# Where the sums of the sevenfold chunks are made: a hybrid decoder layer on one core

## The chip, the core and the metric

The kernel runs on one core of one Trainium2 chip. The time is the device time of one execution in microseconds (us), and the figure compared is the median of several runs. TensorE is written PE (its weight loads PEld), VectorE DVE, ScalarE ACT, GpSimd POOL, SyncE SP. Everything is computed in float32. A DMA that SP or ACT issues is on that engine's queue; the transfers of all queues run on the same 16 DMA engines of the core.

## The reference

One decoder layer for 256 tokens and a model width of 2048. Cut to what matters:

```python
def reference(x, ...):
    h = rmsnorm(x, norm_mix_pre)
    proj = h @ w_in                        # 2048 -> xr, yr, q, k, v, two gates
    y_rnn = rg_lru(conv(xr)) * gelu(yr)
    y_att = sliding_window_sink_attention(rope(q), rope(k), v, sinks)   # 32 heads of 64, 4 kv heads
    mix = sigmoid(g_rnn) * (y_rnn @ w_rnn_proj) + sigmoid(g_attn) * (y_att @ w_attn_proj)
    x = x + rmsnorm(mix @ w_out, norm_mix_post)
    h = rmsnorm(x, norm_mlp_pre)
    u = square(relu(h @ w_mlp_up))         # 2048 -> 8192
    return x + rmsnorm(u @ w_mlp_down, norm_mlp_post)   # 8192 -> 2048
```

## The kernel before, in words

**Weights as a stream.** Every weight matrix is cut into chunks of 128 partitions x 2048 floats (1 MB). `Stream` (from line 52) brings the chunks one after another, in halves of 1024 columns: `load_to` issues a half's DMA on SP's queue (L73) into a buffer `wraw` (four of them, 512 KB each), and `split_to` makes two parts of it, a high part `whi` (ACT, L91) and the low rest `wlo` (DVE, L92), since PE multiplies in three products of two-part numbers: high x high, high x low, low x high. Six halves of parts exist at a time. A `wraw` buffer is free for the next load when its `wlo` is made.

**Stages.** Three input projections with attention and the recurrence between them (to about 735 us), the projection `w_out` with the norms behind it (to about 850 us), then twice (f = 0, 1): up projection, 16 pairs of chunks (`a_pair`, L234 and L237), and down projection in two passes of 1024 output columns (`down`, `n` = 0, 1; matmuls at L908). The last pass ends with the norm and the output.

**Sevenfold chunks.** A chunk of the down projection multiplies a 256 x 256 block of `u` (2 x 2 tiles of 128 x 128) with a 256 x 1024 block of weights (2 x 2 tiles of 128 x 512). The plain way has 8 tile products, 24 matmuls of 512 columns. For the chunks in `SEVEN` (0, 2, 4, 6, 8, 10, 12 of 16 in each of the four passes, 28 in all) a scheme with 7 products of sums of tiles is used, 21 matmuls. The sums of `u`'s tiles are made once by `evacuate` (L888 to L903). The sums of the weights' tiles are made by DVE when the chunk's turn comes (`split_sums`): three additions (L104, L106, L107) make four sums, one of them in place; then come the splits of the chunk's two halves (L91, L92) and of the 1536 columns beside them (ACT L110, DVE L111).

**Attention.** For each of 4 groups of heads and each of two blocks of tokens, the scores `sc` are matmuls over 64 rows: the even heads lie in partitions 0 to 63, the odd ones in 64 to 127. All matmuls of one half (`par`) come first, then those of the other (L527).

**What sets the order.** A scheduler lays out each engine's instructions by data dependencies and the order in which the code is traced. `tc.issue_after(i)` orders what is traced inside behind instruction `i` if both are on one engine, and adds no wait.

Of the kernel before, what the change touches and what calls it, by code (L numbers as in the profile page):

```python
# [16 lines left out]
F32 = mybir.dt.float32  # L17
# [17 lines left out]
WRAW, WHALF, T2, HELD = 4, 6, 8, 4  # L35

SEVEN = (0, 2, 4, 6, 8, 10, 12)
PAIRS = 16
# [13 lines left out]
class Stream:  # L52
# [3 lines left out]
    def __init__(self, nc, pool, chunks, room, sums):  # L56
        self.nc, self.pool, self.chunks, self.room, self.sums = nc, pool, chunks, room, sums
        self.raw, self.parts = {}, {}
        self.loaded = self.split = 0
        self.pin = lambda i: i  # L60
        self.at = 0

    def load_to(self, n):
        while self.loaded < min(n, 2 * len(self.chunks)):
            j = self.loaded
            c = slice(j % 2 * 1024, j % 2 * 1024 + 1024)
            if j < 2 * EXTRA:
                if j % 2 == 0:
                    self.place = self.room(f"wraw{j}")
                t = self.place[:, c]  # L70
            else:
                t = self.pool.tile([P, 1024], F32, tag="wraw", bufs=WRAW, name=f"wraw{j}")
            self.nc.sync.dma_start(t, self.chunks[j // 2][:, c])  # L73
            self.raw[j] = t
            self.loaded += 1

    def split_to(self, n):
        while self.split < min(n, 2 * len(self.chunks)):
            j = self.split
            if j // 2 in self.sums:  # L80
                self.split_sums(j)
                self.split += 2
                continue
            self.load_to(j + 1)
            self.parts[j] = self.two_parts(self.raw.pop(j), j)
            self.split += 1

    def two_parts(self, src, j):
        hi = self.pool.tile([P, 1024], F32R, tag="whi", bufs=WHALF, name=f"whi{j}")
        lo = self.pool.tile([P, 1024], F32R, tag="wlo", bufs=WHALF, name=f"wlo{j}")  # L90
        self.pin(self.nc.scalar.copy(hi, src))  # L91
        self.pin(self.nc.vector.tensor_tensor(lo, src, hi.bitcast(F32), ALU.subtract))  # L92
        return hi, lo

    def split_sums(self, j):


        self.load_to(j + 2)
        v = self.nc.vector
        a, b = self.raw.pop(j), self.raw.pop(j + 1)  # L100
        t = self.room(f"t{j}")[:, 0:1536]
        hi, lo = [self.room(f"t{part}{j}").bitcast(F32R)[:, 0:1536] for part in ("hi", "lo")]
        one, two, l, r = t[:, 0:1024], t[:, 1024:1536], slice(0, 512), slice(512, 1024)
        v.tensor_tensor(one.rearrange("p (a b) -> p a b", a=2), b[:, l].unsqueeze(1).to_broadcast([P, 2, 512]),  # L104
                        a.rearrange("p (a b) -> p a b", a=2), ALU.add)
        v.tensor_tensor(b[:, l], t[:, l], a[:, r], ALU.add)  # L106
        v.tensor_tensor(two, b[:, l], b[:, r], ALU.add)  # L107
        ahi, alo = self.two_parts(a, j)
        bhi, blo = self.two_parts(b, j + 1)
        self.nc.scalar.copy(hi, t)  # L110
        v.tensor_tensor(lo, t, hi.bitcast(F32), ALU.subtract)  # L111
        parts = {"B11": (ahi[:, l], alo[:, l]), "B22": (ahi[:, r], alo[:, r]), "T2": (bhi[:, l], blo[:, l]),
                 "B21": (bhi[:, r], blo[:, r])}
        for i, name in enumerate(("T1", "T3", "T4")):
            c = slice(i * 512, i * 512 + 512)
            parts[name] = hi[:, c], lo[:, c]
        self.parts[j] = parts

    def ahead(self, j):
        self.split_to(j + AHEAD)  # L120
        self.load_to(max(2 * EXTRA, j + WHALF) + WRAW)

    def half(self, run_ahead=True):
        j = self.at
        self.at += 1
        if run_ahead:
            self.ahead(j)
        else:
            self.split_to(j + 1)
        return self.parts.pop(j)  # L130

    def seven(self):

        j = self.at
        self.at += 2
        self.ahead(j)
        return self.parts.pop(j)
# [4 lines left out]
AHEAD = 6  # L142
HELD_LAST = 5
# [6 lines left out]
def layer(tc, x, pos_t, pos_row, inv_freq, vecs, sinks, gains, w_kv, w_q, w_xy, w_rg, w_g, w_rp, w_ap, w_out,  # L150
# [9 lines left out]
    pairs = [psa, psa]  # L160

# [22 lines left out]
    chunks += [w_out[i] for i in range(16)]  # L184
    sums = set()
    for f in range(2):
        chunks += [w_up[32 * f + i] for i in range(32)]
        for n in range(2):
            sums.update(len(chunks) + i for i in SEVEN)
            chunks += [w_dn[(2 * f + n) * PAIRS + i] for i in range(PAIRS)]  # L190

# [6 lines left out]
    ws = Stream(nc, wpool, chunks, lambda name: flat(unit(name, F32)), sums)  # L198
# [25 lines left out]
    def a_pair(acts, out):  # L224


        ps = pair("ps")
        for f in range(2):
            both = ps[:, f].rearrange("p a b -> p (a b)")
            for half in range(2):  # L230
                hi, lo = ws.half()
                act = [acts[kt // 4][:, kt % 4] for kt in range(half * 8, half * 8 + 8)]
                for k, a in enumerate(act):
                    mm(both, hi[:, k * P : k * P + P], a.rearrange("p a b -> p (a b)"),  # L234
                       start=half == 0 and k == 0, stop=False)
                for k, a in enumerate(act):
                    mm(ps[:, f, 1, :], lo[:, k * P : k * P + P], a[:, 0, :], start=False,  # L237
                       stop=half == 1 and k == 7)
                pump()
        nc.scalar.copy(out, ps[:, :, 1, :])  # L240
        nc.vector.tensor_tensor(out, ps[:, :, 0, :], out, ALU.add)

# [13 lines left out]

    def b_pass512(acts, name):

        banks = [[bank(psb, f"{name}{tb}")] for tb in range(TB)]
        for j in range(8):  # L260
            hi, lo = ws.half()
            for i in range(2):
                c = slice(i * 512, i * 512 + 512)
                b_step(banks, acts, 2 * j + i, hi[:, c], lo[:, c], 2 * j + i == KT - 1)
            if j % 2:
                pump()
        return [b[0] for b in banks]
# [31 lines left out]
    def quarter(q):  # L299
        return slice(q * 512, q * 512 + 512)  # L300

    for q in range(4):
        last = nc.sync.dma_start(x_nat[0][:, quarter(q)], x_v[0][:, quarter(q)])
    with tc.issue_after(last.ins):
        ws.load_to(2)
        for q in range(4):
            last = nc.sync.dma_start(x_nat[1][:, quarter(q)], x_v[1][:, quarter(q)])
    with tc.issue_after(last.ins):
        ws.load_to(2 * EXTRA + WRAW)
# [56 lines left out]
    def kv_step(j, hi, lo, tbs):  # L366
        for i in range(2):
            c = slice(i * 512, i * 512 + 512)
            b_step(kv, hT, 2 * j + i, hi[:, c], lo[:, c], 2 * j + i == KT - 1, tbs)
# [14 lines left out]
    held = [ws.half(False) for j in range(2)]  # L384
# [5 lines left out]
    kv_step(0, *held[0], (0,))  # L390
# [5 lines left out]
    kv_step(1, *held[1], (0,))  # L396
# [8 lines left out]
    kv_step(0, *held[0], (1,))  # L405
# [5 lines left out]
    kv_step(1, *held[1], (1,))  # L411
    for j in range(2, 8):
        if j == 4:
            ws.pin = lambda i: i
        kv_step(j, *ws.half(), (0, 1))
# [80 lines left out]
    def attention(g, banks):  # L496
# [11 lines left out]
        for tb in range(TB):  # L508
# [12 lines left out]
            for par in range(2):  # L521
                r0 = par * HD
                for j in range(4 // per):
                    ps = bank(psm, "sc")
                    for i in range(per):
                        h = j * per + i
                        mm(ps[:, i * w : i * w + w], qT[r0 : r0 + HD, h, tb * P : tb * P + P],  # L527
                           kT[r0 : r0 + HD, g, 0:w], start=True, stop=True)
                    at = par * 4 + j * per
# [24 lines left out]
            for par in range(2):  # L554
                for kb in range(nk):
                    ps = bank(psm, "pt")
                    for h in range(4):
                        s3, at = tiles[par * (4 // per) + h // per]
# [94 lines left out]
    def gates(m):  # L653
        hold = []
        for n in (2 * m, 2 * m + 1):
            hi, lo = ws.half()
# [103 lines left out]
    away = ctx2.enter_context(tc.tile_pool(name="away", bufs=1, space=bass.MemoryType.DRAM))  # L760
# [16 lines left out]
    def b_pass1024(acts, n_kt, name, finish, n_held=HELD):  # L777

        banks = [[bank(psb, f"{name}{tb}{i}") for i in range(2)] for tb in range(TB)]
        for kt in range(n_kt - n_held):  # L780
            hi, lo = ws.half()
            b_step(banks, acts, kt, hi, lo, False)
        held = [(kt,) + ws.half(False) for kt in range(n_kt - n_held, n_kt)]
# [6 lines left out]
        if name == "o1":  # L790
            with tc.issue_after(order[1, AFTER][0]), tc.issue_after(order[1, AFTER][1]):
                ws.ahead(ws.at - 1)
        else:
            ws.ahead(ws.at - 1)
# [92 lines left out]
    def evacuate(p, u, dst):  # L887
# [3 lines left out]
        if p not in SEVEN:  # L891
# [13 lines left out]
    def product(b, a, w, begun, tail=False):  # L905

        for i, (x, y) in enumerate(((0, 0), (0, 1), (1, 0))):
# [3 lines left out]
    LEFT = {"P1": (0, "B11"), "Q3": (6, "B22"), "P2": (2, "B21"), "P6": (5, "T2"), "Q4": (1, "T4"), "Q5": (4, "T1"),  # L911
            "N7": (3, "T3")}
# [3 lines left out]
    def down(f, n, uT, held, order, finish, early):  # L916
# [8 lines left out]
        def step(p, parts, names):  # L925
            for name in names:
                at, n2 = name
                b = PLACE[name]
                for i, (hi, lo) in enumerate(parts):
# [198 lines left out]
```

## Time and profile before

| | |
|---|---|
| Median of 3 runs | 1554.8 us (1554.32 to 1557.64) |
| The profiled execution, its own time | 1553.58 us |
| Its span in the profile | 1551.8 us |
| Mean granted PE clock | 0.993 |
| Instructions | 20974 |
| Time busy: PE, DVE, ACT | 1525.7, 1117.5, 843.9 us |
| Bytes moved by DMA | 296.26 MB, mean 191 GB/s |

The profile is of one execution. Its page gives busy times, DMA queues, the chain of work that ended last and the groups of instructions by line; the trace behind it answers for single stretches (windows: busy time per engine, DMA share and GB/s) and for single instructions (timeline: start, duration, engine, line, shape). Matmul durations overlap, since one starts before the one ahead has drained: what a matmul costs is read from the distance of two starts.

### The profile page before, as it was taken

How to read it: one execution, taken by the hardware profiler on the slowest of the kernel's cores; microseconds unless marked ns; L12 is line 12 of the kernel's file. 1: busy time of each engine (PE TensorE's matmuls, PEld its weight loads, DVE VectorE, ACT ScalarE, POOL GpSimd, SP SyncE). 2: the span in 40 equal slices, each digit the busy share in tenths (PEclk: the TensorE clock that was granted, in tenths of full speed). 3: DMA queues.
4: the chain of work that ended last, by engine and by line, in shares of the span. 5: the costliest groups of instructions: out<-in, count | busy, mean ns of one | idle time of the engine just before them, and what ended most of it. 6: DMA issues, size and time to landing. Idle time of an engine off the chain costs nothing.

```text
span 1551.8 us, 20974 instructions
## 1 busy us (share of the span) xinstructions
PE 1525.7 (98%) x8042; PEld 1295.5 (83%) x8042; DVE 1117.5 (72%) x1364; ACT 843.9 (54%) x1156; POOL 1.7 (0%) x9
## 2 busy tenths in 40 slices
PE   8999999999999999999999999999999999999997
PEld 6887777888888888888787888888888888888885
DVE  6666666866859877555655866688886666788997
ACT  5555545646647766444344655555454555555553
POOL 0000000000000000000000000000000000000000
PEclk9999999999999999999999999999999999999999
DMA  6554354354655465555663855556666655566664
GB/s 246 188 169 148 115 173 147 124 191 149 229 188 177 158 213 198 190 184 190 250 221 98 278 190 189 187 175 213 218 203 218 221 187 189 188 242 232 203 216 138
DMA packets 82902, 296.26 MB, mean 191 GB/s; under 512 B 9585, under 2 KB 9841, under 8 KB 81777
## 3 DMA queue, kind: packets, MB, share of 16 engines
q1 hardware_dynamic: 79344, 285.48, 55.7%
q10 hardware_dynamic: 3458, 9.45, 1.6%
q8 instruction: 63, 1.03, 0.3%
q14 instruction: 37, 0.30, 0.1%
HBM read 288.60 MB, written 6.29 MB: 190 GB/s over the span
## 4 chain that ended last, share of the span: by engine, by line
PE 87%; DVE 5%; ACT 3%; DMA 3%; issue 2%; SPq 0%; DVEq 0%; ACTq 0%
PE ps L234 36%; PE ps L237 18%; PE dQ L908 7%; PE s L908 4%; PE dP L908 3%; DVE wlo L92 2%; PE dCs L908 2%; DMA wraw<-in_w_dn 2%; PE o L251 2%; PE o L255 2%; PE o L253 2%; PE q L251 2%; PE q L253 2%; PE q L255 2%; PE sc L527 1%
## 5 line engine op out<-in xcount | busy, mean ns | idle before, releaser
L92 DVE TENSOR_TENSOR wlo<-wraw,whi 128x1024 fp32r<-128x1024 f32 x528 | 639.8, 1221 | 322.4 <-ACT whi L91 317.0
L91 ACT CAST whi<-wraw 128x1024 fp32r<-128x1024 f32 x528 | 549.0, 1049 | 585.9 <-PE ps L234 271.5
L234 PE MATMUL ps<-hT,whi 128*128 128x512 f32 x1024 | 260.5, 394 | 0.0
L234 PE MATMUL ps<-h2T,whi 128*128 128x512 f32 x1024 | 258.2, 394 | 0.5 <-DVE h2T L280 0.5
L234 PEld LDWEIGHTS ps<-hT,whi 128*128 128x128 f32 x1024 | 183.8, 189 | 36.5 <-issue 3.5
L234 PEld LDWEIGHTS ps<-h2T,whi 128*128 128x128 f32 x1024 | 185.3, 190 | 34.2 <-DVE h2T L280 0.9
L237 PEld LDWEIGHTS ps<-hT,wlo 128*128 128x128 f32 x1024 | 140.1, 190 | 11.7 <-issue 2.0
L237 PEld LDWEIGHTS ps<-h2T,wlo 128*128 128x128 f32 x1024 | 140.0, 191 | 10.1
L237 PE MATMUL ps<-hT,wlo 128*128 128x256 f32 x1024 | 145.3, 283 | 0.0
L237 PE MATMUL ps<-h2T,wlo 128*128 128x256 f32 x1024 | 143.0, 283 | 0.0
L908 PE MATMUL dQ<-whi,uT 128*128 128x512 f32 x288 | 106.5, 389 | 0.0
L234 PE MATMUL ps<-yrnn,whi 128*128 128x512 f32 x256 | 64.4, 393 | 0.7 <-DVE yrnn L700 0.7
L234 PE MATMUL ps<-yatt,whi 128*128 128x512 f32 x256 | 64.1, 392 | 0.0
L908 PEld LDWEIGHTS dQ<-whi,uT 128*128 128x128 f32 x288 | 54.1, 188 | 11.2
L908 PE MATMUL dQ<-wlo,uT 128*128 128x512 f32 x144 | 56.1, 390 | 1.6 <-DVE wlo L92 1.6
L111 DVE TENSOR_TENSOR tlo<-t,thi 128x1536 fp32r<-128x1536 f32 x28 | 49.2, 1757 | 10.1 <-ACT thi L110 10.1
L908 PE MATMUL dP<-whi,uT 128*128 128x512 f32 x144 | 53.8, 389 | 0.0
L908 PE MATMUL dCs<-whi,uT 128*128 128x512 f32 x144 | 53.7, 389 | 0.0
L234 PEld LDWEIGHTS ps<-yrnn,whi 128*128 128x128 f32 x256 | 46.0, 189 | 9.3 <-DVE yrnn L700 1.1
L234 PEld LDWEIGHTS ps<-yatt,whi 128*128 128x128 f32 x256 | 46.0, 189 | 8.2
L251 PE MATMUL q<-whi,hT 128*128 128x512 f32 x128 | 51.1, 399 | 0.0
L253 PE MATMUL q<-wlo,hT 128*128 128x512 f32 x128 | 50.2, 392 | 0.0
(251 smaller groups left out, 2068.6 us busy)
## 6 DMA issues: line engine op xcount, KB each, us to landing
wraw<-in_w_up SPq DMA_DIRECT2D x128, 512.0 KB, 4.6
wraw<-in_w_dn SPq DMA_DIRECT2D x128, 512.0 KB, 4.5
wraw<-in_w_g SPq DMA_DIRECT2D x64, 512.0 KB, 4.4
wraw<-in_w_xy SPq DMA_DIRECT2D x64, 512.0 KB, 3.9
wraw<-in_w_q SPq DMA_DIRECT2D x32, 512.0 KB, 4.3
wraw<-in_w_ap SPq DMA_DIRECT2D x32, 512.0 KB, 3.8
wraw<-in_w_rp SPq DMA_DIRECT2D x32, 512.0 KB, 4.6
wraw<-in_w_out SPq DMA_DIRECT2D x32, 512.0 KB, 4.8
```

Source lines behind the costliest of these rows:

```text
L91: self.pin(self.nc.scalar.copy(hi, src))
L92: self.pin(self.nc.vector.tensor_tensor(lo, src, hi.bitcast(F32), ALU.subtract))
L111: v.tensor_tensor(lo, t, hi.bitcast(F32), ALU.subtract)
L234: mm(both, hi[:, k * P : k * P + P], a.rearrange("p a b -> p (a b)"), start=half == 0 and k == 0, stop=False)
L237: mm(ps[:, f, 1, :], lo[:, k * P : k * P + P], a[:, 0, :], start=False, stop=half == 1 and k == 7)
L251: mm(banks[tb][n], a[:, 0, t], hi[:, n * 512 : n * 512 + 512], start=first, stop=False)
L253: mm(banks[tb][n], a[:, 0, t], lo[:, n * 512 : n * 512 + 512], start=False, stop=False)
L255: mm(banks[tb][n], a[:, 1, t], hi[:, n * 512 : n * 512 + 512], start=False, stop=last)
L527: mm(ps[:, i * w : i * w + w], qT[r0 : r0 + HD, h, tb * P : tb * P + P], kT[r0 : r0 + HD, g, 0:w], start=True, stop=True)
L908: mm(b, a[x], w[y], start=not begun and i == 0, stop=tail and i == 2)
```

## The change

1. **Sums in DRAM.** The seven operands of a sevenfold chunk are now loaded as two pieces: three quarters as they are (1536 columns, from the weights) and four sums (2048 columns) from a DRAM room `sums`. POOL's queue fills the rooms, two chunks to a group, 22 groups: six copies, two accumulating transfers of 1024 columns, and in the two later steps an accumulating transfer of 512 columns each for both chunks. `split_sums` and its additions on DVE are gone.
2. **44 sevenfold chunks, not 28**: 10 of 16 in each pass of f = 0, 12 of 16 in each pass of f = 1. More of their `u` sums lie in the units of the pool `big`.
3. **Splits on whole pieces.** Loads still are DMAs of at most 1024 columns, but a raw buffer holds a piece (2048 columns, two of them, in the down passes two more from `big`), three pieces of parts exist, and for the up and down projection one instruction splits a whole piece.
4. **Beside it:** scores of even and odd heads alternate matmul by matmul; the last pair of each up projection is evacuated at a higher priority; loads of the residual and the last gain are moved on ACT's queue, and the multiplication by the gain is spread over the last pass.

```diff
-WRAW, WHALF, T2, HELD = 4, 6, 8, 4
-SEVEN = (0, 2, 4, 6, 8, 10, 12)
+T2, HELD = 8, 2
+SEVEN = ((0, 1, 3, 4, 6, 7, 9, 10, 12, 13), (0, 1, 2, 3, 4, 5, 7, 8, 9, 10, 11, 12))
+IN_UNITS = (3, 5)
...
+PARTS, RAW = 3, 2
+EVERY = 7
...
+    def load(self):
+        if self.loaded == len(self.pieces):
+            return False
+        j = self.loaded
+        loads, w, step, own = self.pieces[j]
+        if self.waits[own] == (EXTRA if j < EXTRA else RAW):
+            return False
+        t = self.room(f"wraw{j}") if own else self.pool.tile([P, 2048], F32, tag="wraw", bufs=RAW, name=f"wraw{j}")
+        for c, src in loads:
+            self.nc.sync.dma_start(t[:, c], src)
...
     def split_to(self, n):
...
+            if j not in self.parts:
+                self.parts[j] = [self.pool.tile([P, 2048], F32R, tag=tag, bufs=PARTS, name=f"{tag}{j}")
+                                 for tag in ("whi", "wlo")]
+            src = self.raw[j]
+            hi, lo = self.parts[j]
+            i = self.pin(self.nc.scalar.copy(hi[:, c], src[:, c]))
+            self.pin(self.nc.vector.tensor_tensor(lo[:, c], src[:, c], hi[:, c].bitcast(F32), ALU.subtract))
             self.split += 1
...
+            if self.split == len(self.cuts) or self.cuts[self.split][0] != j:
+                del self.raw[j]
+                self.waits[self.pieces[j][3]] -= 1
+                self.each(j, i)
-    def split_sums(self, j):
...
+    def own(at):
+        return at >= 0 and at % 2 == 0
...
     for f in range(2):
+        pieces += [piece(w_up[32 * f + i], step=2048) for i in range(32)]
         for n in range(2):
+            at = -4 if f == 1 and n == 0 else 0
+            for i in range(PAIRS):
+                src = w_dn[(2 * f + n) * PAIRS + i]
+                if i in SEVEN[f]:
...
+                    pieces.append(piece(src, 1536, 2048, own(at)))
+                    pieces.append(piece(sums[f, n, i], 2048, 2048, own(at + 1)))
+                    at += 2
+                else:
+                    pieces.append(piece(src, 2048, 2048, own(at)))
+                    at += 1
...
+    def sums_steps():
+        dma = nc.gpsimd.dma_start
...
+        for i in range(len(groups) + 2):
+            if i >= 2:
+                t, w = groups[i - 2]
+                dma(cols(t, 1536, 2048), cols(t, 1024, 1536), accum_op=ALU.add)
+            if 1 <= i <= len(groups):
+                t, w = groups[i - 1]
+                dma(cols(t, 1024, 1536), cols(t, 0, 512), accum_op=ALU.add)
+            if i < len(groups):
+                t, w = groups[i]
+                for k, src in enumerate(w):
+                    dma(t[k][:, 1024:2048], src[:, 512:1536])
+                    dma(t[k][:, 0:512], src[:, 1536:2048])
+                    dma(t[k][:, 512:1024], src[:, 1536:2048])
+                for k, src in enumerate(w):
+                    dma(t[k][:, 0:1024], src[:, 0:1024], accum_op=ALU.add)
+            yield
...
+    def each(j, i):
+        if j % EVERY == 0 and j >= EVERY and pieces[j][0][0][1].tensor.name != w_dn.tensor.name:
+            with tc.issue_after(i.ins):
+                next(summing, None)
...
-            for par in range(2):
-                r0 = par * HD
-                for j in range(4 // per):
-                    ps = bank(psm, "sc")
-                    for i in range(per):
-                        h = j * per + i
+            for j in range(4 // per):
+                both = [bank(psm, "sc") for par in range(2)]
+                for i in range(per):
+                    h = j * per + i
+                    for par in range(2):
+                        r0 = par * HD
...
-            a_pair(h2T, wide(u))
+            a_pair(h2T, wide(u), PRIO if p == PAIRS - 1 else 0)
```

**POOL's queue.** Before, POOL has nothing but constants and masks, and its last rows of work are these (Pool_49 is its own semaphore):

```order
masks.py:197 MEMSET ident 128x128
L428 MEMSET mask_392 128x256
masks.py:199 ISA
masks.py:199 AFFINE_SELECT ident<-ident 128x128 [waits Pool_49]
L430 AFFINE_SELECT mask_392<-mask_392 128x256 [waits Pool_49]
L432 AFFINE_SELECT mask_392<-mask_392 128x256 [waits Pool_49]
```

Now the transfers start among the masks, at the program's beginning. Here is the end of the first group's copies with what follows (L221 to L223 copy, L225, L217 and L214 add; DMASW0 to DMASW7 are the semaphores of POOL's own transfers):

```order
L223 DMA sums0_69<-in_w_dn 128x512
L225 DMA sums0_69<-in_w_dn 128x1024 [waits DMASW2_49,DMASW1_49]
L221 DMA sums1_70<-in_w_dn 128x1024
L225 DMA sums0_69<-in_w_dn 128x1024 [waits DMASW5_49,DMASW4_49,DMASW0_49]
L222 DMA sums1_70<-in_w_dn 128x512
L223 DMA sums1_70<-in_w_dn 128x512
L221 DMA sums1_70<-in_w_dn 128x1024 [waits DMASW3_49]
L217 DMA sums0_69<-sums0_69 128x2x512 [waits DMASW6_49,DMASW0_49]
```

All 220 transfers of this queue wait for semaphores of that kind alone; none waits for ACT, whose instruction `each` hands to `issue_after`.

**The scores on PE.** Before, in the first group of heads (the first two rows are block 0 of the tokens, the others block 1; `ps` and `q10` are projections that run beside it):

```order
L527 MATMUL sc_912<-kT_428,qT0_816 128x128 x4
L527 MATMUL sc_919<-kT_428,qT0_816 128x128 x4
...
L527 MATMUL sc_1032<-kT_428,qT0_816 128x256 x2
L234 MATMUL ps_945<-hT3_141,whi31_859 128x512 x2
L237 MATMUL ps_945<-hT2_140,wlo31_860 128x256
L527 MATMUL sc_1037<-kT_428,qT0_816 128x256 x2
```

Now, at the same places:

```order
L566 MATMUL sc_902<-kT_431,qT0_815 128x128
L566 MATMUL sc_903<-kT_431,qT0_815 128x128
L566 MATMUL sc_902<-kT_431,qT0_815 128x128
L566 MATMUL sc_903<-kT_431,qT0_815 128x128
...
L566 MATMUL sc_1022<-kT_431,qT0_815 128x256 x2
L274 MATMUL ps_935<-hT3_163,wlo15_853 128x256 x4
L287 MATMUL q10_1061<-whi16_936,hT0_160 128x512
L289 MATMUL q10_1061<-wlo16_937,hT0_160 128x512
L566 MATMUL sc_1023<-kT_431,qT0_815 128x256 x2
```

In block 0 the two halves alternate in all four groups of heads; of block 1's eight pairs only one in each of the second and third group stands alternating, the others are laid out one behind the other, as here.

More of the change, by code (lines that the diff above doesn't have):

```diff
@@ L52, with __init__ @@
 class Stream:
-    def __init__(self, nc, pool, chunks, room, sums):
-        self.nc, self.pool, self.chunks, self.room, self.sums = nc, pool, chunks, room, sums
+    def __init__(self, nc, pool, pieces, room):
+        self.nc, self.pool, self.pieces, self.room = nc, pool, pieces, room
         self.raw, self.parts = {}, {}
-        self.loaded = self.split = 0
+        self.loaded = self.split = self.at = 0
+        self.cuts = [(j, slice(c, min(c + step, w))) for j, (loads, w, step, own) in enumerate(pieces)
+                     for c in range(0, w, step)]
@@ L77, in split_to @@
-    def split_to(self, n):
[L78 to L85, printed above, removed]
-            self.split += 1
[L88 to L93, printed above, removed]
@@ L95, in split_sums @@
-    def split_sums(self, j):
[L98 to L123, printed above, removed]
+        self.each = lambda j, i: None
+        self.waits = [0, 0]
+    def load(self):
[8 more added lines that the diff above has]
+            self.nc.sync.dma_start(t[:, c], src)
+        self.raw[j] = t
+        self.waits[own] += 1
+        self.loaded += 1
+        return True
@@ L124, in half, with ahead, next @@
+    def ahead(self, last):
+        self.split_to(sum(j <= last for j, c in self.cuts))
+        while self.load():
+            pass
+    def next(self, run_ahead=True):
         j = self.at
         self.at += 1
[L126 to L136, printed above, removed]
+        self.ahead(j + PARTS - 1 if run_ahead else j)
         return self.parts.pop(j)
@@ L160, in layer @@
     pairs = [psa, psa]
+    away = enter(tc.tile_pool(name="away", bufs=1, space=bass.MemoryType.DRAM))
     mm = nc.tensor.matmul
@@ L308, in layer @@
     with tc.issue_after(last.ins):
[L309 removed]
+        while ws.load():
+            pass
     ident = const.tile([P, P], F32, name="ident")
@@ L414, in layer @@
             ws.pin = lambda i: i
-        kv_step(j, *ws.half(), (0, 1))
+        ws.split_to(j + 3)
+        kv_step(j, (0, 1))
+    for j in range(4):
+        ws.next()
     pos_i = pa.tile([P, TB], I32, name="pos_i")
@@ L654, in gates @@
         hold = []
+        both = ws.next()
         for n in (2 * m, 2 * m + 1):
-            hi, lo = ws.half()
+            hi, lo = [t[:, n % 2 * 1024 : n % 2 * 1024 + 1024] for t in both]
             xc, xs, th = rnn.pop(n)
```

231 lines of the change are left out of this document (119 added, 112 removed).

## The prediction

> **What bounds the kernel now.** I read the page's busy times first, then the chain that ended last, then single stretches.
>
> ```profile
> span 1551.8 us, 20974 instructions
> PE 1525.7 (98%) x8042; PEld 1295.5 (83%) x8042; DVE 1117.5 (72%) x1364; ACT 843.9 (54%) x1156; POOL 1.7 (0%) x9
> PE 87%; DVE 5%; ACT 3%; DMA 3%; issue 2%; SPq 0%; DVEq 0%; ACTq 0%
> q1 hardware_dynamic: 79344, 285.48, 55.7%
> q10 hardware_dynamic: 3458, 9.45, 1.6%
> ...
> HBM read 288.60 MB, written 6.29 MB: 190 GB/s over the span
> ```
>
> PE is busy 98% of the span and carries 87% of the chain: the kernel ends when PE has done its matmuls, and everything else counts only where it makes PE wait. PE's waits in the stage that changes are small:
>
> ```profile
> PE s L908 <- DVE u L241: 1.9, 2, 1.1
> PE dQ L908 <- DVE wlo L92: 1.6, 1, 1.6
> ```
>
> That is the start of each first down pass, and once inside. So a gain must be matmuls taken away, and a loss a new wait of PE.
>
> The rows q1 and q10 are SP's and ACT's queues: 57.3% of the DMA engines' time between them. What the engines give when SP's queue is full shows in the first three of these windows (the last two columns are DMA share and GB/s), what the weights need in the others:
>
> ```profile
> 8.00:12.00 4.00, 2.56 (x6) 0.78 (x5) 0.66 (x3) 1.59 (x4) 0.00 (x0) 1.00 1.02 371
> 12.00:16.00 4.00, 2.59 (x11) 1.62 (x11) 3.54 (x5) 3.09 (x7) 0.00 (x0) 0.72 1.04 416
> ...
> 24.00:28.00 4.00, 4.00 (x21) 3.29 (x20) 4.00 (x6) 1.81 (x3) 0.00 (x0) 1.00 1.01 391
> 0.00:320.00 320.00, 312.47 (x1603) 250.91 (x1604) 216.38 (x346) 176.92 (x333) 1.70 (x9) 0.99 0.50 165
> 320.00:735.00 415.00, 414.27 (x2435) 366.28 (x2434) 286.52 (x338) 246.26 (x325) 0.00 (x0) 1.00 0.57 188
> ```
>
> 416 GB/s is the ceiling seen, 165 and then 188 the need: a bit under half of it.
>
> **The change, part by part.** The base is the profiled execution's own 1553.6 us (span 1551.8 and 1.8 around it); the median of the three runs is 1.2 us more.
>
> *Matmuls.* The starts of a sevenfold chunk, of the plain one behind it and of the next:
>
> ```profile
> 1396.82 0.39 PE L908 MATMUL s<-whi,seven 128*128 128x512 f32 x1
> ...
> 1401.58 0.39 PE L908 MATMUL dQ<-whi,uT 128*128 128x512 f32 x1
> ...
> 1407.02 0.39 PE L908 MATMUL s<-whi,seven 128*128 128x512 f32 x1
> ```
>
> 21 matmuls take 4.76 us and 24 take 5.44, so one costs 0.227 us. 44 - 28 = 16 chunks lose three each: 48 x 0.227 = **-10.9 us**, on the path throughout.
>
> *Scores.* Two halves of PE's rows take turns now. The trace has no such case, but one beside it: `po` alternates between halves of the columns, `gain_b` (also f32, 512 columns) does not alternate.
>
> ```profile
> 6.83 3.73 PE L339 MATMUL gain_b<-gain,ones 128*128 128x512 f32 x8 [0.28 <-DMA gain<-in_gains]
> 138.94 1.94 PE L567 MATMUL po<-pT,v_sb 128*64 128x512 f32 x8
> 100.43 1.71 PE L527 MATMUL sc<-kT,qT 64*128 64x128 f32 x16
> 118.35 1.99 PE L527 MATMUL sc<-kT,qT 64*128 64x256 f32 x8
> ```
>
> Eight take 3.73 us one after the other and 1.94 alternating: they run side by side. Of the scores, the four block-0 sets (the third row, 1.71 us each) and two of the eight block-1 pairs (the last row, 1.99 us each) stand alternating. Halving them all would give 4 x 0.85 + 2 x 1 = 5.4 us; nothing at all is the other end, or a microsecond lost, since a pair now wants both PSUM banks at once. I take **-3**, a little nearer to what `po` shows.
>
> *Start of the down passes.* The priority for the last evacuation addresses the first of the two waits above, 1.9 us; bounds 0 to -3.5. I take **-2**.
>
> *DVE and ACT.* The rows of one chunk's weights:
>
> ```profile
> L92 DVE TENSOR_TENSOR wlo<-wraw,whi 128x1024 fp32r<-128x1024 f32 x528 | 639.8, 1221 | 322.4 <-ACT whi L91 317.0
> L91 ACT CAST whi<-wraw 128x1024 fp32r<-128x1024 f32 x528 | 549.0, 1049 | 585.9 <-PE ps L234 271.5
> L111 DVE TENSOR_TENSOR tlo<-t,thi 128x1536 fp32r<-128x1536 f32 x28 | 49.2, 1757 | 10.1 <-ACT thi L110 10.1
> L110 ACT CAST thi<-t 128x1536 fp32r<-128x1536 f32 x28 | 41.4, 1479 | 14.6 <-DVE t L107 8.3 <-PE s L908 6.2
> L104 DVE TENSOR_TENSOR t<-wraw,wraw 128x1024 f32<-128x1024 f32 x28 | 34.2, 1223 | 9.9 <-DMA wraw<-in_w_dn 9.2 <-PE dQ L908 0.3
> L107 DVE TENSOR_TENSOR t<-wraw 128x512 f32<-128x512 f32 x28 | 19.3, 691 | 0.9
> ```
>
> Before, DVE spends 2 x 1.22 + 1.76 + 1.22 + 2 x 0.69 = 6.8 us on a sevenfold chunk. After, it splits 1536 and 2048 columns; 512 more columns cost 0.54 on DVE and 0.43 on ACT, so 2048 take 2.29 and 1.91: DVE 4.05, ACT 3.39 per chunk of 4.76 on PE. Where six such chunks stand in a row (f = 1) DVE is at 85%. The additions that go were hidden behind PE, so they give nothing: 0. What is late next is the split itself: with three buffers of parts, a 2048 piece is begun when the piece three ahead of it is done and must be ready 4.76 us later; it takes 1.91 + 2.29 = 4.2. The slack is half a microsecond, and whatever else DVE has to do at the passes' ends eats it. Bounds 0 and 10 us (0.2 us on each of 48 pieces of f = 1); I take **+2**.
>
> *Loads of the down passes.* Per pass they are 10 x 1.84 + 6 x 1.05 = 24.6 MB in 80 us (f = 0) and 26.2 MB in 79 us (f = 1): 307 and 332 GB/s, against the 416 ceiling. A sevenfold chunk's pieces are wanted every 2.38 us on average, and four raw buffers serve them.
>
> ```profile
> wraw<-in_w_dn SPq DMA_DIRECT2D x128, 512.0 KB, 4.5
> SPq L73 <- DVE wlo L92: 1129.4, 466, 22.9
> ```
>
> A buffer is held for the landing (4.5 us, more when the engines are full), then for the split (4.2 or 3.2): 8.2 to 10 us, over four buffers 2.05 to 2.5. That is just enough or just not; SP's wait for `wlo`, harmless now, is the row that would matter. 0.12 us on each of the 88 pieces of sevenfold chunks would be 11 us. Bounds 0 and 11; I take **+2**.
>
> *Making the sums.* 44 chunks copy 1.05 MB and add 1.05 MB each: 92 MB. The order shows that nothing paces them: POOL starts at once and runs as fast as its own transfers land. Beside the first loads (the engines are full from 8 to 28 us already) that delays the first weights: bounds 0 and 10 us (half of those 20), I take **+2**, since POOL begins with its masks. From then on the question is how many packets the weights get. Nearest rows: SP's queue at 416 GB/s; ACT's queue, over half of it writes to DRAM (most of the 6.29 MB written are its own), 9.45 MB in 1.6% of 1551.8 us, 24.8 us, or 381 GB/s. By these a copy costs the engines as much as a load, an addition, which reads two streams, twice. Taking turns packet by packet, the weights get 208 GB/s beside copies and 139 beside additions. Per group: 2.1 MB of copies, 10 us, 0.2 MB gained over the need of 188; 2.1 MB of additions, 15 us, 0.74 MB short; between them two landings with the engines to the weights alone, some 4 us, 0.9 MB gained. It closes, and 2 MB of raw buffers carry the swing: **0**, with the other end in the rivals.
>
> The Trainium skill (Collectives: The Full Stack, the bandwidth ceiling) says that an addition in the DMA engines is slower because it needs two source reads, 32 against 62 GB/s; by that the factor is the 2 taken here. No run here shows it yet.
>
> Sum: -10.9 - 3 - 2 + 2 + 2 + 2 = -9.9, so 1553.6 - 9.9 = 1543.7: I forecast **1544**. Its own range from the bounds that are likely together: 1534 to 1552.
>
> **The rivals.**
> *The additions starve the weights (slower).* If an addition costs three packets (two reads, one write, nothing overlapped), the weights get 104 GB/s for 20 us a group, 1.7 MB short, against 1.1 MB gained: 0.6 MB, 3.2 us of PE for each group. A group then lasts 34 us; nine fall before 320 us, where 165 GB/s are enough; 13 remain: 42 us, and more where buffers run dry in between. 1586 to 1620, I take 1600. It decides near 2.3 packets an addition. For it: no pacing, and a queue that is 220 transfers deep. Against: POOL's own waits, which leave holes.
> *Copies cost two packets as well (slower still).* Then 139 GB/s beside the copies too, 15 us, 0.74 MB short instead of 0.2 gained: 1.5 MB or 8 us of PE a group, 22 groups: 1544 + 100 to 180, about 1690. The Trainium skill (DMA: Bandwidth & Descriptors, latency and other measured facts) has copies within HBM at 207 to 214 GB/s per direction, half of the 416 here; by that rule this rival would come. The trace has no such copy.
> *The down passes become bound by their raw buffers (about the same).* +10 instead of +2 there, and +2 more at the splits: 1554.
> *The halves of PE's rows don't run side by side.* 1547, still faster; it is inside the forecast's range.
>
> **How the numbers follow.** Forecast 0.58; additions starve 0.20; copies too 0.12; down passes bound 0.10. A measurement of this kernel tells 0.2%, some 3 us, from no change. The third rival is "same"; of the forecast nearly all lies under 1551.7: faster 0.57, same 0.10, slower 0.33. The range leaves out the second rival and the end of the first: low 1530 (every gain at its bound and no cost is 1534; the runs' own spread of 3 us comes on top), high 1640.
>
> **What would show it.** Matmuls at L955 and the rest: 7887 against 7935 in the program, and PE's busy time lower by about 13. Right: POOL's transfers end before 800 us, the window 320 to 735 shows SP's weights still at 188 GB/s and PE busy over 99%; `po`-like spacing (0.055 and 0.12 us) in the alternating scores. Wrong: PE waiting for `wlo` or `whi`, these for DMA `wraw` of the projection stages, with a landing time several times 4.5 us; or the same wait at L955 from 1370 us on, without any transfer of POOL's beside it.

## The result and the profile after

The changed kernel takes **1761.0 us** (median of 4 runs, 1759.0 to 1767.7) beside 1554.6 us before: a ratio of **1.1335**, 95% interval 1.1298 to 1.1372. Forecast were 1544 us and a range of 1530 to 1640. The profiled execution took 1761.4 us. Times are medians over a kernel's fast runs; the one slow run, the fourth of e7 below (1711.7 us), is left out.

The page after, in the lines that answer to those shown of before, with its 40 slices of PE's granted clock and of the DMA engines' share (tenths):

```profile
span 1759.6 us, 20688 instructions
PE 1576.2 (90%) x7994; PEld 1321.6 (75%) x7994; DVE 1078.4 (61%) x1200; ACT 851.0 (48%) x1052; POOL 163.3 (9%) x229
...
PEclk8989898989799897889999999999999999999998
DMA  9999999999999999956557537565989765578795
...
q1 hardware_dynamic: 91728, 319.04, 53.2%
q0 software_dynamic: 31680, 92.29, 26.3%
q10 hardware_dynamic: 3602, 10.50, 1.6%
...
HBM read 415.47 MB, written 98.57 MB: 292 GB/s over the span
...
PE 51%; DMA 30%; DVE 9%; ACT 6%; issue 2%; SPq 1%; DVEq 0%; ACTq 0%
```

PE, busy 98% before, is busy 90%, and the chain that ended last runs through DMA for 30% where it was 3%. The second row of slices gives the place: 17 slices of 44 us each in which the DMA engines never rest, and then the picture of before. The new row is q0, POOL's queue. The same two windows as before (the last two columns are DMA share and GB/s, the third from the end is the granted clock):

```profile
0.00:320.00 320.00, 268.86 (x1264) 210.63 (x1265) 166.52 (x249) 138.71 (x258) 71.90 (x106) 0.91 0.99 256
320.00:735.00 415.00, 331.91 (x1764) 281.90 (x1763) 226.47 (x312) 183.58 (x274) 88.62 (x121) 0.89 1.00 247
```

The engines are full at 250 GB/s, although 416 was the most that they had moved before. PE idles 134 us in the two together, where it idled 8.3 us before. Who gets the time, in the queues' rows for the stretch from 0 to 760 us:

```profile
q0 software_dynamic: 31534, 92.02, 60.6%
q1 hardware_dynamic: 28080, 97.76, 38.0%
```

POOL's transfers take 60.6% of the engines, SP's weights 38.0%: 97.76 MB in 760 us, 129 GB/s, where 165 and then 188 were needed. The landing times of the loads, by tensor, say the same (before, the first of them read 3.9):

```profile
wraw<-in_w_xy SPq DMA_DIRECT2D x64, 512.0 KB, 10.9
wraw<-in_w_ap SPq DMA_DIRECT2D x32, 512.0 KB, 11.2
wraw<-in_w_up SPq DMA_DIRECT2D x128, 512.0 KB, 4.7
```

`w_xy` and `w_ap` are loaded beside POOL, `w_up` after it. And PE waits for what the late splits have delayed, most of all the gates' chain (`room`):

```profile
PE pg L709 <- ACT room L714: 54.8, 4, 16.2
PE ps L272 <- ACT whi L96: 27.1, 15, 5.3
```

The first and last start (behind the comma) of the matmuls that read `h2T` (the two up projections), before and after:

```profile
L234 PE MATMUL ps<-h2T,whi x1024: 387/389/797, 849.4 to 1373.8; 128*128 128x512 f32 x171
```

```profile
L272 PE MATMUL ps<-h2T,whi x1024: 387/393/796, 1047.2 to 1567.0; 128*128 128x512 f32 x171
```

The down passes of f = 0 and f = 1, from their first matmul to the one behind them, or to their last; first before, then after:

```profile
1030.55 0.40 PE L908 MATMUL s<-whi,seven 128*128 128x512 f32 x1
...
1196.23 1.98 PE L234 MATMUL ps<-h2T,whi 128*128 128x512 f32 x8
...
1374.97 0.40 PE L908 MATMUL s<-whi,seven 128*128 128x512 f32 x1
...
1542.67 0.39 PE L908 MATMUL dQ<-whi,uT 128*128 128x512 f32 x1
```

```profile
1228.01 0.40 PE L955 MATMUL s<-whi,seven 128*128 128x512 f32 x1
...
1389.42 1.98 PE L272 MATMUL ps<-h2T,whi 128*128 128x512 f32 x8
...
1568.16 0.40 PE L955 MATMUL s<-whi,seven 128*128 128x512 f32 x1
...
1747.86 0.39 PE L955 MATMUL dQ<-whi,uT 128*128 128x512 f32 x1
```

With these rows the 207.8 us between the two spans divide as follows.

| Stretch | before | after | difference |
|---|---|---|---|
| start to the first up projection | 849.4 | 1047.2 | +197.8 |
| up projection f = 0 | 181.2 | 180.8 | -0.3 |
| down passes f = 0 | 165.7 | 161.4 | -4.3 |
| up projection f = 1 | 178.7 | 178.7 | 0 |
| down passes f = 1 | 168.1 | 180.1 | +12.0 |
| tail | 8.7 | 11.4 | +2.6 |

There are two losses: one of 198 us beside POOL's transfers, and one in the down passes of f = 1, where ten chunks of three matmuls less should have given 6.8 us and 12.0 came on top: 18.8 us.

### The profile page after: what moved, and what is told of

It reads as the page before. It is cut to its first block, busy times and chain, and to the rows that moved or that the text cites. A ratio compares the mean times of both kernels' runs of the same rounds, so it can differ in the third digit from the quotient of the medians.

```text
span 1759.6 us, 20688 instructions
## 1 busy us (share of the span) xinstructions
PE 1576.2 (90%) x7994; PEld 1321.6 (75%) x7994; DVE 1078.4 (61%) x1200; ACT 851.0 (48%) x1052; POOL 163.3 (9%) x229
## 3 DMA queue, kind: packets, MB, share of 16 engines
q0 software_dynamic: 31680, 92.29, 26.3%
## 4 chain that ended last, share of the span: by engine, by line
PE 51%; DMA 30%; DVE 9%; ACT 6%; issue 2%; SPq 1%; DVEq 0%; ACTq 0%
PE ps L272 20%; PE ps L274 10%; DMA wraw<-in_w_xy 8%; DMA wraw<-in_w_ap 5%; DMA wraw<-in_w_g 5%; DVE wlo L97 5%; PE dQ L955 5%; PE s L955 4%; ACT whi L96 4%; DMA wraw<-in_w_q 3%; DMA wraw<-in_w_rg 3%; PE dP L955 2%; DMA wraw<-sums 2%; PE o L287 2%; PE o L289 2%
## 5 line engine op out<-in xcount | busy, mean ns | idle before, releaser
L97 DVE TENSOR_TENSOR wlo<-wraw,whi 128x1024 fp32r<-128x1024 f32 (+2 forms) x444 | 695.7, 1583 | 509.3 <-ACT whi L96 507.5
L96 ACT CAST whi<-wraw 128x1024 fp32r<-128x1024 f32 (+2 forms) x444 | 588.4, 1339 | 660.0 <-PE ps L272 134.5
L272 PE MATMUL ps<-hT,whi 128*128 128x512 f32 x1024 | 277.9, 413 | 13.4 <-ACT whi L96 13.4
L955 PE MATMUL s<-whi,seven 128*128 128x512 f32 x352 | 125.9, 398 | 3.1 <-ACT whi L96 3.1
L955 PEld LDWEIGHTS s<-whi,seven 128*128 128x128 f32 x352 | 67.8, 193 | 17.8 <-ACT whi L96 3.5
L955 PE MATMUL s<-wlo,seven 128*128 128x512 f32 x176 | 71.1, 404 | 5.0 <-DVE wlo L97 5.0
L709 PE MATMUL pg<-xs,whi 128*128 128x256 f32 x64 | 23.0, 360 | 57.5 <-ACT room L714 54.8
L955 PE MATMUL dQ<-whi,seven 128*128 128x512 f32 x176 | 68.4, 396 | 1.3 <-ACT whi L96 1.3
L955 PE MATMUL dQ<-whi,uT 128*128 128x512 f32 x160 | 58.2, 391 | 1.2 <-ACT whi L96 1.2
L225 POOL DMA_DIRECT2D sums<-in_w_dn x44 | 37.5, 853 | 177.0 <-issue 135.9
## 6 DMA issues: line engine op xcount, KB each, us to landing
wraw<-in_w_xy SPq DMA_DIRECT2D x64, 512.0 KB, 10.9
```

The lines of the kernel that those rows point to most:

```text
L96: i = self.pin(self.nc.scalar.copy(hi[:, c], src[:, c]))
L97: self.pin(self.nc.vector.tensor_tensor(lo[:, c], src[:, c], hi[:, c].bitcast(F32), ALU.subtract))
L225: dma(t[k][:, 0:1024], src[:, 0:1024], accum_op=ALU.add)
L709: mm(dst, hi[:, c], xs[:, k, 0, :], start=k == 0, stop=False)
L955: mm(b, a[x], w[y], start=not begun and i == 0, stop=tail and i == 2)
```

## The experiments

Ratios are to runs of the kernel before on the same chip.

### Is it the making of the sums, and what does each kind of transfer cost?

**e1_no_making**

```diff
-                    pieces.append(piece(sums[f, n, i], 2048, 2048, own(at + 1)))
+                    pieces.append(piece(src, 2048, 2048, own(at + 1)))
...
-    ws.each = each
```

> Leaves out the making of the sums (POOL issues none of its 220 transfers); the second piece of a sevenfold chunk is loaded from the weights instead, the same bytes. Theory M (POOL's unpaced transfers fill the DMA engines until 760 us and cost the 198 us by which the changed kernel is late when its first up projection begins): that delay goes. What is left is 1553.6 - 10.9 (48 matmuls) - 2.2 (four sets of scores, 0.55 us each) - 2 + 19 (lost inside the down passes of f = 1) + 3 (tail) = about 1560, 1550 to 1568. Theory L (the new form of the loads, pieces of 2048 columns in two raw buffers, makes the projections late): at least 1650, whatever POOL does.

Measured: 1562.6 us, ratio 1.0067 (1.0041 to 1.0093). The first up projection begins at 848.6 us instead of 1047.2. That is theory M: the 198 us come with the making. What stays is slower than before by 8 to 9 us, and lies in the down passes of f = 1 (1368.8 to 1548.8 us, 180.0).

**e2_copies_only** leaves out the three calls with `accum_op`; **e3_adds_as_copies** keeps them without it (one of the three):

```diff
-                dma(cols(t, 1536, 2048), cols(t, 1024, 1536), accum_op=ALU.add)
+                dma(cols(t, 1536, 2048), cols(t, 1024, 1536))
```

> Leaves out the 88 accumulating transfers that read the weights and the 44 + 44 sums of sums; the 132 copies of POOL's (46 MB) stay. POOL's 92 MB took 460 us of all 16 engines. Price P1 (a copied byte costs what a loaded one does, 1/338 us per KB; the additions cost the rest): copies take 136 us of the engines, at a share of 62% they last 220 us, the weights get 129 GB/s in them instead of some 171: 9 MB short, about 50 us lost: 1610. Price P2 (a copied byte costs as much as an added one): 230 us of the engines, 370 us long, about 85 us lost: 1645. Theory L: at least 1740, since POOL matters little.

(Of the 88 accumulating transfers, in fact, 44 read the weights and 22 and 22 add sums to sums, each for two chunks.)

> All 220 transfers stay, with the same shapes and waits, but the additions are plain copies (so the sums are wrong values). P1: 272 us of the engines instead of 460, the copying lasts 440 us, about 100 us lost: 1660. P2: nothing changes, 1755 to 1765, POOL's last transfer at 750 to 770 us.

Measured: e2 1618.5 us (1.0426, 1.0394 to 1.0458), e3 1684.0 us (1.0837, 1.0800 to 1.0873). Both are nearer to price P1, a copy as cheap as a load, e2 by 8 us and e3 by 24 above it. POOL's queue in e2, then in e3, over the whole span (1622.6 and 1675.1 us):

```profile
q0 software_dynamic: 13376, 46.15, 8.8%
```

```profile
q0 software_dynamic: 26048, 92.29, 19.8%
```

Share times span is the time of all 16 engines, and differences between the kernels give the single kinds (estimates from the rows):

| Transfer | MB | engine time, us | GB/s |
|---|---|---|---|
| SP's loads (changed kernel, 0 to 760 us) | 97.8 | 289 | 338 |
| POOL's copies (e2) | 46.15 | 143 | 323 |
| the additions' shapes, as copies (e3 less e2) | 46.14 | 189 | 244 |
| the additions (changed kernel less e2) | 46.14 | 320 | 144 |

The queues' rows while POOL was at work show something else. First e2 from 0 to 236 us, then e3 from 0 to 560:

```profile
q0 software_dynamic: 13031, 44.99, 59.1%
q1 hardware_dynamic: 9792, 31.56, 39.0%
```

```profile
q0 software_dynamic: 25720, 91.13, 58.6%
q1 hardware_dynamic: 22022, 75.72, 39.7%
```

31.56 MB in 236 us are 134 GB/s, 75.72 in 560 are 135, and the changed kernel had 129. So beside a full queue of POOL's, with these raw buffers, the weights get 0.38 to 0.40 of the engines whatever POOL's transfers cost. The price only sets how long the queue stays full: 240, 560 or 760 us. Each microsecond of that costs PE what is missing from the need (177 GB/s on average: 130.07 MB from 0 to 735 us before): for the changed kernel 760 x (1 - 129/177) = 206 us, where 198 were measured. The same estimate gives 58 us for e2 and 133 for e3; beyond e1 they lost 56 and 121.

### What sets the 0.39, and does pacing help?

**e4_paced_fine** issues one transfer for each piece split (two at every eighth), behind a mark that ACT writes and a small copy of POOL's reads; a group's sums of sums now come right behind its other transfers:

```diff
+            mark = const.tile([P, 1], F32, tag="mark", bufs=16, name=f"mark{j}")
+            nc.scalar.copy(mark, ws.parts[j][0][:, 0:1].bitcast(F32))
+            seen = const.tile([P, 1], F32, tag="seen", name=f"seen{j}")
+            with tc.issue_after(nc.gpsimd.tensor_copy(seen, mark).ins):
+                for _ in range(2 if j % TWICE == 0 else 1):
+                    next(summing, None)
```

> The whole work stays; POOL now issues one transfer (two at every eighth piece) each time ACT has split a piece of the projections, through a small copy that reads a mark which ACT writes. Theory M, in the form that it is the share while POOL's queue is never empty: one transfer is 2.1 us of the engines on average for each piece of 5.6 us; the weights get 129 GB/s for some 3.4 us of it and up to 338 in the rest, 211 on average against 188 needed: nothing is lost in the projections, 1560, at most 1580. If it is the sheer amount of bytes instead, wherever they come: 1700 or more. Theory L: 1700 or more as well.

Measured: 1705.1 us (1.0959, 1.0889 to 1.1029). 56 us less than unpaced, but a miss by 145 us: the share while POOL is active is not all. The engines now have time left, yet PE still loses (the columns after the window: PE, PEld, DVE, ACT, POOL):

```profile
480.00:640.00 160.00, 133.72 (x762) 118.12 (x760) 107.04 (x141) 96.27 (x158) 34.49 (x47) 0.91 0.74 204
```

A quarter of the engines' time is free there, and the weights are late. SP's weights in this window, and what SP itself waited for longest:

```profile
q1 hardware_dynamic: 6131, 22.34, 41.4%
SPq L80 <- DVE wlo L97: 105.4, 22, 16.2
```

For 105.4 of the 160 us SP waits for a split to give a raw buffer back (before, in the same window, for 133.8, but there the weights were in time). The loads also land later beside POOL's transfers; `w_xy` in e1, without them, and in e4:

```profile
wraw<-in_w_xy SPq DMA_DIRECT2D x64, 512.0 KB, 4.7
```

```profile
wraw<-in_w_xy SPq DMA_DIRECT2D x64, 512.0 KB, 7.4
```

The most that SP has on its way are two raw pieces, 2.1 MB. If a buffer's round (landing, waiting, split) takes 11 us, that is some 190 GB/s, the need; 16 us make 131. By this estimate the 22.34 MB of the window, 140 GB/s, are a round of 15 us. In the kernel before, the same 2.1 MB were four buffers, each free for its next load when its own half was split. So the next three kernels put that back: unpaced (**e7_halves**), paced (**e8_halves_paced**) and without the making (**e9_halves_no_making**). Their common edit, besides splits of 1024 columns everywhere (in the projections the splits had that size already, so there only the buffers change):

```diff
-        t = self.room(f"wraw{j}") if own else self.pool.tile([P, 2048], F32, tag="wraw", bufs=RAW, name=f"wraw{j}")
-        for c, src in loads:
-            self.nc.sync.dma_start(t[:, c], src)
+        for k, (c, src) in enumerate(loads):
...
+                half = self.pool.tile([P, 1024], F32, tag="wraw", bufs=2 * RAW, name=f"wraw{j}_{k}")[:, 0:w]
+            self.nc.sync.dma_start(half, src)
```

> The changed kernel with its making unpaced, but raw buffers of 1024 columns again, four of them, each free for its next load when its own half is split (the parts stay whole pieces; all splits are of 1024 columns). Theory A (the engines' time is shared: beside POOL's full queue SP's loads get 0.38 to 0.40 of it, which is 130 GB/s, whatever waits behind): 1755 to 1765 as before. Theory B (SP has at most 2 MB on its way, and a buffer's round, landing of 11 us and split, sets the 130 GB/s): a buffer's round shortens from some 16 to 13 us, 155 to 160 GB/s, about half of the 200 us comes back: 1640 to 1690.

> The finely paced kernel (1705 us) with the same four raw buffers of 1024 columns. There the engines are busy 74 to 89% of the projections, so bandwidth is left over, and the loads land in 7.5 us, not 4.7. Theory B (buffer rounds): most of the loss goes, 1570 to 1640. Theory A (shares alone): 1690 to 1710.

> Control: no making of the sums, four raw buffers of 1024 columns. Beside the kernel with whole-piece buffers (1562.6 us) the projections have nothing to gain, since loads land in 4.7 us there; only the passes of f = 1 could, if it is buffers and not bandwidth that holds them: by theory D 1558 to 1565, by buffer rounds 1545 to 1555.

Measured: e7 1682.2 us (three runs; 1.0879, 1.0814 to 1.0943), e8 1618.0 (1.0406, 1.0378 to 1.0433), e9 **1543.3** (0.9936, 0.9917 to 0.9955). The same bytes in the same buffer space, returned by halves: 79 us less unpaced, 87 less paced, 19 less without the making. Theory A falls. Theory B has the direction, and e7's time lies in its range, but the rate that it foresaw is too high: the queues' rows of e7 from 0 to 690 us

```profile
q0 software_dynamic: 28165, 82.54, 57.9%
q1 hardware_dynamic: 28047, 97.65, 42.1%
```

give the weights 142 GB/s, not 155 to 160. How much of the share is set by the loads on their way and how much by the order in which the engines serve the two queues stays open; a kernel with more bytes on the way was not run.

**e10_halves_paced_copies** and **e11_marks_only** take e8 apart: additions as copies, and pacing without POOL's transfers.

> The paced kernel with four raw buffers of 1024 columns (1618 us, 75 us above the same without the making), with its additions replaced by plain copies of the same shapes (the sums are wrong values): 332 us of engine time for POOL instead of 462. If what is left of the loss is the engines' fullness (83 to 98% busy from 320 us on), it falls by more than half: 1560 to 1585. If it is POOL's presence, whatever its transfers cost: 1605 to 1620.

> Control for the pacing: four raw buffers of 1024 columns, ACT's marks and POOL's small copies stay, POOL's 220 transfers are left out and the second pieces are loaded from the weights. If the pacing itself costs nothing, it is the kernel without it, 1543, at most 1547; if the marks on ACT and POOL's copies beside DVE cost part of the 75 us: 1555 or more.

Measured: e10 1561.9 us (1.0060, 1.0042 to 1.0077), e11 1542.2 (0.9938, 0.9919 to 0.9957). Marks cost nothing; e8's 75 us are its transfers, and 56 of them the additions' price over that of copies. The same window in e8, then in e10 (which is 20 to 30 us further in the program there):

```profile
640.00:800.00 160.00, 150.29 (x834) 131.24 (x833) 88.95 (x90) 72.16 (x108) 43.28 (x61) 0.97 0.93 284
```

```profile
640.00:800.00 160.00, 156.81 (x834) 135.47 (x833) 91.17 (x97) 69.30 (x106) 47.46 (x58) 0.98 0.84 281
```

The engines move as many bytes, within 1%, in a share of 0.93 and of 0.84, and PE idles 9.7 us in the first and 3.2 in the second.

### The down passes of f = 1

**e6_half_loads** (on e1) loads half of each second piece in f = 1 and splits it twice:

```diff
+            if len(self.pieces[j][0]) == 1:
+                a = src[:, 0:1024].unsqueeze(1).to_broadcast([P, 2, 1024])
```

> The kernel without the making of the sums (1562.6 us), in which in addition the second piece of a sevenfold chunk of f = 1 is loaded by half (1024 columns, split twice): 0.52 MB less for each of the 24 chunks, with every matmul and every split as it was. Without the making, the two passes of f = 1 last 180 us where 168.1 - 6.8 = 161 were due, and the DMA engines are busy 93 to 98% at 335 to 345 GB/s where sevenfold chunks follow one another. Theory D (loads: 12 sevenfold chunks and a plain one are 23.1 MB in 62.6 us, 369 GB/s): with 268 GB/s the 18.6 us come back, 1544, at most 1548. Theory S (splits: 4.2 us of every 4.76 on DVE and ACT in three buffers of parts): 1558 to 1563.

Measured: 1549.9 us (0.9979, 0.9965 to 0.9993). That is above theory D's 1548 and below theory S's 1558. The passes last 169.2 us, 10.8 less than in e1, with every split as it was: more than half of the 18.7 us hang on the loads. But the engines' bandwidth is not the limit either, as e9 shows with all its loads. One window of the sevenfold stretch in e1, then in e9:

```profile
1400.00:1440.00 40.00, 38.47 (x167) 30.88 (x166) 30.04 (x15) 25.39 (x15) 0.00 (x0) 1.00 0.96 341
```

```profile
1400.00:1440.00 40.00, 40.00 (x179) 33.10 (x178) 31.90 (x32) 27.40 (x32) 0.00 (x0) 1.00 0.98 366
```

e1 stands at a DMA share of 0.96 and 341 GB/s and looks full; e9, with buffers that return earlier, moves 366 there (381 from 1480 to 1520 us), and PE loses nothing in this window. Its passes last 166.0 us, 14.0 less than in e1, although a half of `w_dn` lands in 6.7 us there and in 6.0 in e1. Theory D as I put it, bandwidth, falls; a shorter hold of the buffers fits. But in these passes e9 also splits 2048 columns in two steps where e1 takes one, and the two were not separated. Some 5 us to the 161.3 due remain.

### The two parts that cost no transfer

**b1_scores** is the kernel before with the alternating scores, **b2_scores_prio** adds the priority:

```diff
-            a_pair(h2T, wide(u))
+            a_pair(h2T, wide(u), PRIO if p == PAIRS - 1 else 0)
```

> The kernel before, with one part of the change alone: the scores of even and odd heads alternate. In the trace of the changed kernel a set of 16 scores of block 0 takes 1.16 us where it took 1.71. Forecast's term: 3 us less than before, a ratio of 0.998; by the trace of the changed kernel 4 x 0.55 = 2.2 us less, 0.9986. If the rows' halves gained nothing in the end, because what waits for the scores is late anyway: 1.000.

> The kernel before with the alternating scores and the higher priority of the last pair's evacuation: the two parts of the change that cost no transfer. Forecast's terms: 3 + 2 us less, a ratio of 0.997. If both are worth nothing: 1.000. Either way PE should show no wait for u at the start of the down passes.

Measured: b1 1550.9 us (0.9986, 0.9975 to 0.9997), b2 1553.9 us (0.9998, 0.9984 to 1.0011). The scores are worth about 2 us, as their rows say; the first set of block 0 in b1:

```profile
99.83 1.16 PE L527 MATMUL sc<-kT,qT 64*128 64x128 f32 x16
```

The priority is worth nothing that shows. PE's waits in b2:

```profile
PE dQ L911 <- DVE wlo L92: 6.6, 3, 5.4
...
PE s L911 <- DVE u L242: 0.3, 1, 0.3
```

The wait for `u` fell from 1.9 to 0.3 us (it is 1.2 in b1, without the priority), and the one for `wlo` near the end of the last pass stood at 6.6 instead of 1.6. It is 4.4 in b1 without the priority, so most of it does not come from the priority; why it differs was not tried. Of the kernels that do the whole work, b1 is the only one whose interval lies below 1, by 0.14% (0.03 to 0.25), a difference far too small to call the kernel faster.

## Why the prediction was wrong, point by point

- **Matmuls, -10.9.** Right where nothing else was late: the passes of f = 0 lost 4.3 us for six chunks (4.1 by the term). In f = 1 the 6.8 us were eaten.
- **Scores, -3.** About right: 1.71 to 1.16 us a set, 2 us in all (b1). **Priority, -2.** Wrong: the wait goes, the time does not (b2).
- **Making the sums, 0.** This is the step that failed: "Taking turns packet by packet, the weights get 208 GB/s beside copies and 139 beside additions. [...] It closes". The price taken for a copy was right (323 GB/s by engine time against 338 for loads, a factor of 1.05 for the 1 assumed), that for an addition a little low (338/144 = 2.3, not 2, and 2.3 was the very point that I gave for the rival). Wrong were the turns and the holes. Beside copies alone the weights got 134 GB/s, not 208 (e2), and beside the whole making 129, below even the 139 that were meant for additions alone; and no holes came: POOL's queue and SP's together filled 98.6% of the engines for 760 us. By e2 alone the copies lose 56 us beyond e1 where the forecast had them gain.
- **"2 MB of raw buffers carry the swing."** They can't: with landings of 11 us they are part of the limit themselves. And I had read the third part of the change, the whole pieces, only for the down passes, not for what it does to the same 2.1 MB in the projections. In e7 the first up projection begins at 985.1 us, 62 of the 198 us earlier; the other 136 come with POOL's queue beside these buffers too:

```profile
L278 PE MATMUL ps<-h2T,whi x1024: 387/390/496, 985.1 to 1502.6; 128*128 128x512 f32 x171
```
- **Down passes, +2 and +2** (bounds 10 and 11). The mechanism was there, the size was not: 18.7 us in e1. The term took the landing of before, 4.5 us; in e1 a `w_dn` half lands in 6.0. By that estimate a round is 10.2 us, 2.55 over four buffers where 2.38 are due: 8 us on 48 pieces, not all of it. Besides, the need was averaged over a pass, 332 GB/s; twelve of the first thirteen chunks of f = 1 are sevenfold, 23.1 MB in 62.6 us or 369 GB/s, beside ACT's loads.
- **Start-up, +2** (bounds 0 and 10). Too small. The first `q` matmuls, before and after (first and last start behind the comma):

```profile
L251 PE MATMUL q<-whi,hT x128: 389/389/504, 66.5 to 262.9; 128*128 128x512 f32 x128
```

```profile
L287 PE MATMUL q<-whi,hT x128: 388/390/629, 88.2 to 323.5; 128*128 128x512 f32 x128
```

22 us were lost by 66.5 us of the old time: the start is a part of the one loss of 198 us, and no small end beside it.

**The rivals.** "The additions starve the weights" (1600) named what happened; its price of three packets was too high, and its arithmetic kept the turns and the holes. "Copies cost two packets as well" came nearest in time (1690), but by luck: e2 refutes its mechanism, and its 1.5 MB a group leave out the 0.9 MB from the holes that the first rival counts; with them it is 0.6 MB, some 3 us a group, and at most about 1610. By the engine time here, copies ran at 323 GB/s. The Trainium skill (DMA: Bandwidth & Descriptors, latency and other measured facts) has 207 to 214 GB/s, measured with rows 512 KiB and more apart on SP's or ACT's queue; here the rows are 8 KB apart on POOL's, and no run shows its case. The weights' share of the engines was 0.38 to 0.40, and 0.42 in the projections with nothing changed but the buffers (e7). The Trainium skill's rule for two queues (DMA: Bandwidth & Descriptors, queues, rings and completion order), that each engine takes turns between them by packets, leaves open what share comes out. One sign told nothing: POOL's transfers did end before 800 us (92.02 of 92.29 MB by 760), as they were to do if the forecast was right. "PE busy lower by about 13" was wrong as well: it rose by 50 us.

## What to carry to other kernels

A stream that hides its loads behind a fixed number of buffers can move no more than the buffers' bytes in each round, landing plus hold. A second stream that lengthens the landing can then slow it even while the DMA engines have time to spare, as in e4 (landings of 7.4 us instead of 4.7, a DMA share of 0.74). So ask of added traffic what it does to the landing time before adding up bytes. Try buffers cut as finely as the work that frees them: halves were worth 19 to 87 us here. And look for what really holds a queue back: `issue_after` on another engine's instruction held back nothing here, and the unpaced queue took its share from the start.

## What the runs showed that I had not expected

- An accumulating transfer between DRAM and DRAM takes 1.7 times the engine time of a plain copy of the same shape (320 against 189 us for 46 MB).
- A DMA share near 1 is no measure of bandwidth here: 250 GB/s beside POOL's transfers, 341 in e1 and 381 in e9 all stand at 0.96 to 1.00.
- PE's clock was lower where it waited in between: its granted clock was 0.91 and 0.89 in the two windows where it was starved, 0.99 and 1.00 before. The mean of its largest group of matmuls, which counts the longer ones right behind a wait too, went from 394 ns to 413 (before, then after):

```profile
L234 PE MATMUL ps<-hT,whi 128*128 128x512 f32 x1024 | 260.5, 394 | 0.0
```

```profile
L272 PE MATMUL ps<-hT,whi 128*128 128x512 f32 x1024 | 277.9, 413 | 13.4 <-ACT whi L96 13.4
```
